# The last stage of a DeltaNet and mLSTM layer takes the mLSTM's product first

## The chip, the cores and the metric

One core of a Trainium2 chip runs the whole program once. The metric is the device time of that execution in microseconds; smaller is better. Three runs of the kernel before gave 989.99, 992.57 and 992.75 us, with a median of 992.57 us. One further execution was taken with the hardware profiler; its time and its trace are used below.

## What is computed

One layer of a backbone over 512 latent tokens (in a row behind 256 context tokens), with 1024 channels. Two mixers read one input projection: a bidirectional gated DeltaNet of 8 heads, whose gated output is `ya`, and a bidirectional mLSTM of 4 heads, whose gated output is `yb`. The part that matters here is the end of the layer:

```
ya = rmsnorm(oa) * silu(z_a)
yb = rmsnorm(hb) * sigmoid(o_b) * silu(z_b)
y  = sigmoid(g_a) * (ya @ w_pa) + sigmoid(g_b) * (yb @ w_pb)
x  = x + gate * (y @ w_out)
out = rmsnorm(x, final_g)
```

`ya` and `yb` are 512 x 1024, and the three weights are 1024 x 1024. The gates `g_a` and `g_b` come from the input projection too, 1024 columns each: 16 dense products of 128 columns, numbered 0 to 15, of which 0 to 7 gate the `ya` product and 8 to 15 the `yb` product.

## The kernel before

Every dense product is done in split precision. A weight chunk of 1024 x 128 is loaded into one of two `raw` buffers (512 KB, queue of SP), ACT casts it into one of three slots of `whs` (line 753, the high part), and DVE subtracts to get `wls` (line 754, the low part). Data has a high and a low part in the same way. One product of 128 columns for 512 tokens is then 24 matmuls of 128x512: for each of 8 blocks of the inner dimension `kt` high by high (line 768), low by high (769) and high by low (770), all into one of two PSUM banks `psd`. A bank is free for the product after next once ACT or DVE has read it.

The mixers come first. Their instructions are not issued as written: a recorder collects them (in the trace they all have line 460), and a list scheduler with a table of costs of its own orders them for each engine. Fillers such as the gate products are handed to it by stretches of a head; the list `G` (line 1529) says how many gate products each of the eight stretches gets. `g_dense` makes one: weights, 24 matmuls, a tanh on ACT into the tile `sg`, and a store of 256 KB to the scratch tensor `sg_d` in DRAM. One gate product is made before the heads and one after the last head, so 14 of the 16 are made there. The last head writes its part of `ya` to `ya_d` and the last mLSTM head its two blocks of `yb` to `yb_d` (scratch in DRAM too).

The last stage (from line 1572 on) is issued as written, though the framework interleaves the engines and gives each engine a fixed order. It has four pieces:

- It loads the 8 blocks of `yb`, then the 8 blocks of `ya`, 256 KB each, into tiles `yld` of which there are three (lines 1585 and 1586), casts each on ACT (line 1587, `ybh` or `yah`) and subtracts on DVE (line 1588, `ybl` or `yal`). A load into a `yld` tile waits until DVE has subtracted from its former tenant.
- `g_last` makes the gate products that are left (14 and 15) with the tanh on ACT into tiles `sgl` (line 1595) that stay on the chip.
- For each of 8 column chunks `n` it takes the `ya` product with `w_pa` and then the `yb` product with `w_pb`. A gate that is not in `sgl` is loaded from `sg_d` (line 1610, two buffers). DVE multiplies the product by the gate (line 1613, tile `yt`), GpSimd adds the two terms (line 1615), ACT and DVE split the sum into `yh` and `yl`.
- Then comes the product with `w_out` (line 1654) and the final norm.

What decides the order around the change is the queue of SP, which issues all loads and stores one after the other and stops at each that has to wait, and the order of ACT and DVE, which stop at each instruction that has to wait.

Of the kernel before, what the change touches and what calls it, by code (L numbers as in the profile page):

```python
# [10 lines left out]
F32 = mybir.dt.float32  # L11
F32R = mybir.dt.float32r
AF = mybir.ActivationFunctionType
ALU = mybir.AluOpType

P = 128
D = 1024
KT = D // P
T = 512
# [473 lines left out]
def hybrid(tc, x, c, ctx_in, c_ctx, ada_w, ada_b, norm_g, w_in, conv_w, a_log, dt_bias,  # L493
           norm_a_g, i_bias, f_bias, norm_b_g, w_pa, w_pb, w_out, final_g, out):
    nc = tc.nc
# [78 lines left out]
    sg_d = dram.tile([2 * KT, P, T], F32, name="sg_d")  # L574
# [29 lines left out]
    nc = rec  # L604
# [9 lines left out]
    ya_d, yb_d, sg_d, gate_d, rows_d = [rec.wrap(t, "DRAM") for t in (ya_d, yb_d, sg_d, gate_d, rows_d)]  # L614
# [127 lines left out]
    def next_slot(n=1):  # L742
        i = slot[0] % NW
        if i + n > NW:
            i = 0
        slot[0] = i + n
        return i

    def split_w(src, c0, wh, wl):

        raw = wpool.tile([P, KT, P], F32, tag="raw", name="raw", bufs=2)
        nc.sync.dma_start(raw, src[:, c0:c0 + P].rearrange("(kt p) n -> p kt n", p=P))
        nc.scalar.copy(wh, raw)  # L753
        nc.vector.tensor_tensor(wl, raw, wh.bitcast(F32), op=ALU.subtract)  # L754

    def load_w(src, c0, at=None):
        i = next_slot() if at is None else at
        split_w(src, c0, whs[:, i], wls[:, i])
        return whs[:, i], wls[:, i]

    def dense_g(w, rh, rl, t0, t1):

        wh, wl = w
        next(between, None)
        ps = psd()
        o = ps[:, 0:t1 - t0]
        for kt in range(KT):
            nc.tensor.matmul(o, wh[:, kt, :], rh[:, kt, t0:t1], start=kt == 0, stop=False)  # L768
            nc.tensor.matmul(o, wh[:, kt, :], rl[:, kt, t0:t1], start=False, stop=False)  # L769
            nc.tensor.matmul(o, wl[:, kt, :], rh[:, kt, t0:t1], start=False, stop=kt == KT - 1)  # L770
            if kt % 2 and kt < KT - 1:
                yield 6 * (t1 - t0) / 2400
        next(between, None)
        return o

    def dense_ch(*args):
        g = dense_g(*args)
        while True:
            try:
                next(g)  # L780
            except StopIteration as e:
                return e.value
# [3 lines left out]
    def seq(*gens):  # L786
        for g in gens:
            yield from g
# [13 lines left out]
    def weave(*streams):  # L802

        live = [[0.0, cost, g] for cost, g in streams]
        while live:
            st = min(live, key=lambda x: x[0] / x[1])
            try:
                st[0] += next(st[2])
            except StopIteration:
                live.remove(st)  # L810
# [527 lines left out]
    def z_dense(h):  # L1338
        w = load_w(win, O_AZ + P * h)
        pz = yield from dense_g(w, hh, hl, TC, TT)  # L1340
        sz = mx.tile([P, T], F32, tag="sz", name="sz", bufs=2)
        nc.scalar.activation(sz, pz, AF.Silu)
        heads[h]["sz"] = sz
        yield 1.28
# [28 lines left out]
    def ml_dense(j):  # L1373
        w = load_w(win, O_BK + P * j)
        k = mx.tile([P, NLC * DVB], F32, tag="mkH", name="mk")[:, 0:TT]
        sck = float(P) ** -0.5
        o = yield from dense_g(w, hh, hl, TC, TT)
        nc.scalar.activation(k[:, TC:TT], o, AF.Copy, scale=sck)
        yield 1.28
        o = yield from dense_g(w, hh, hl, 0, TC)  # L1380
        nc.scalar.activation(k[:, 0:TC], o, AF.Copy, scale=sck)
        yield 0.64
        w = load_w(win, O_BQ + P * j)
        q = mx.tile([P, T], F32, tag="mq", name="mq")
        o = yield from dense_g(w, hh, hl, TC, TT)
        nc.scalar.copy(q, o)
        yield 1.28
        V = mx.tile([P, NCH, DVB + 4], F32, tag="mV", name="mV")
        nc.gpsimd.memset(V[:, :, DVB:DVB + 1], 1.0)
        i = next_slot(2)  # L1390
        for half in range(2):
            load_w(win, O_BV + DVB * j + P * half, at=i + half)
        for ch0 in range(0, NCH, 2):
            ps = psd()
            n = 0
            for ch in range(ch0, ch0 + 2):
                o = ps[:, DVB * (ch - ch0):DVB * (ch - ch0) + DVB]
                tk = slice(P * ch, P * ch + P)
                for kt in range(KT):
                    for a, b in ((hh, whs), (hh, wls), (hl, whs)):  # L1400
                        nc.tensor.matmul(o, a[:, kt, tk], b[:, i:i + 2, kt, :], start=n == 0, stop=n == 2 * 3 * KT - 1)
                        n += 1
                    if kt % 4 == 3:
                        yield 1.28
            nc.scalar.copy(V[:, ch0:ch0 + 2, 0:DVB], ps.rearrange("p (c i) -> p c i", i=DVB))
        ml[j] = (q, k, V)
# [113 lines left out]
    def g_some(n):  # L1520
        for _ in range(n):
            if gn[0] < 2 * KT:
                gn[0] += 1
                yield from g_dense(gn[0] - 1)
# [1 line left out]
    weave((18, gates_g()), (46, seq(qkv(0), g_some(1), qkv(1))))  # L1526
    weave((W_E + W_KV, seq(dn_kv(0), dn_scores(0))), (20.5, qkv(2)))
    weave((W_A2 + W_E, seq(dn_prepa2(0), dn_scores(1))), (33, seq(z_dense(0), ml_dense(0))))
    G = [0, 4, 0, 4, 0, 4, 0, 0]
    for h in range(HA):  # L1530
        j = h // 2
        last = h + 1 == HA
# [21 lines left out]
        if h + 3 < HA:  # L1554
            de.append(qkv(h + 3))
            cost += 20.5
        if G[h]:
            de.append(g_some(G[h]))
            cost += 5.1 * G[h]
        streams = [(wd, seq(*dn)), (cost, seq(*de))]  # L1560
# [7 lines left out]
    nc, ps_d, ps_l, ps_s, ps_o, wpool, cvp, hh, hl, whs, wls, ya_d, yb_d, sg_d, gate_d, cpow = plain  # L1568
# [10 lines left out]
    mg = mgs.enter_context(tc.tile_pool(name="mg", bufs=1, reuse_waits="tile"))  # L1579
    parts = []  # L1580
    for name, src in (("b", yb_d), ("a", ya_d)):
        ph = mg.tile([P, KT, T], F32R, name=f"y{name}h")
        pl = mg.tile([P, KT, T], F32R, name=f"y{name}l")
        for kt in range(KT):
            t = mg.tile([P, T], F32, tag="yld", name="yld", bufs=3)
            nc.sync.dma_start(t, src[P * kt:P * kt + P, :])
            nc.scalar.copy(ph[:, kt, :], t)  # L1587
            nc.vector.tensor_tensor(pl[:, kt, :], t, ph[:, kt, :].bitcast(F32), op=ALU.subtract)
        parts.append((ph, pl))
    sgl = {}  # L1590
# [10 lines left out]
    wo = [(mr.tile([P, KT, HD], F32R, name="woh"), mr.tile([P, KT, HD], F32R, name="wol"))]  # L1601
    wol1 = mr.tile([P, KT, HD], F32R, name="wol1")
    rf = mr.tile([P, 104], F32, name="rf")[:, 0:NLC]
    for n in range(KT):
        terms = []
        for i, ((ph, pl), wsrc) in enumerate(((parts[1], w_pa[0]), (parts[0], w_pb[0]))):
            g = sgl.get(KT * i + n)
            if g is None:
                g = mg.tile([P, T], F32, tag="sg", name="sg", bufs=2)
                nc.sync.dma_start(g, sg_d[KT * i + n])  # L1610
            w = load_w(wsrc, P * n)
            t = mg.tile([P, T], F32, tag="yt", name="yt", bufs=2)
            nc.vector.scalar_tensor_tensor(t, g, 1.0, dense_ch(w, ph, pl, 0, T), op0=ALU.add, op1=ALU.mult)
            terms.append(t)
        nc.gpsimd.tensor_tensor(terms[0], terms[0], terms[1], op=ALU.add)
        nc.scalar.activation(yh[:, n, :], terms[0], AF.Copy, scale=0.5)
        nc.vector.scalar_tensor_tensor(yl[:, n, :], terms[0], 0.5, yh[:, n, :].bitcast(F32), op0=ALU.mult, op1=ALU.subtract)
# [10 lines left out]
    mg = es.enter_context(tc.tile_pool(name="mo", bufs=1, reuse_waits="tile"))  # L1628
# [17 lines left out]
    n = [0] * NLC  # L1646
    for i, c0, c1 in pieces:
        wh, wl = wo[c0 // HD]
        cs, w0, w = slice(c0, c1), c0 % HD, c1 - c0
# [6 lines left out]
        t = mg.tile([P, HD], F32, tag="ot", name="ot", bufs=2)[:, 0:w]  # L1656
# [42 lines left out]
```

## Time and profile before

| | |
|---|---|
| three runs, us | 989.99, 992.57, 992.75 |
| profiled execution, us | 991.41 |
| its span in the trace, us | 989.7 |
| PE busy | 950.6 us, 96% of the span |
| DVE, ACT, POOL busy | 73%, 55%, 22% |
| mean granted clock of PE | 0.989 |

The profile is that of one execution. Its time (991.41) is 1.7 us more than its span, which is what lies around the program. A busy share is of the whole span; PE is the engine that is nearly always busy, so that a change is looked for in the places where PE is idle, or runs below its full clock. Times in the rows are counted from the start of the span.

### The profile page before, as it was taken

Reading aid. Unit: us, or ns where it says so; the run is one execution under the profiler, and the core shown is the slowest. Engines: PE = TensorE matmul, PEld = TensorE weight load, DVE = VectorE, ACT = ScalarE, POOL = GpSimd, SP = SyncE. Lnnn points to the kernel's source line nnn. Section 1 sums busy time; section 2 is a strip of 40 time slices with the busy share of each in tenths; the row PEclk is TensorE's granted clock in tenths of the full one; section 3 lists DMA queues with packets and bytes.
Section 4 is the critical chain, followed back from the end, with each engine's and each line's share of the span. In section 5 each row is a group of like instructions: output and inputs, shape, how many; then the busy total and the mean of one; then the engine's idle time right before and its main releaser. Section 6 shows DMA issues by size and latency. Waiting matters only on the chain.

```text
span 989.7 us, 15262 instructions
## 1 busy us (share of the span) xinstructions
PE 950.6 (96%) x5504; PEld 814.6 (82%) x5504; DVE 722.8 (73%) x1646; ACT 545.4 (55%) x1226; POOL 215.0 (22%) x292
## 2 busy tenths in 40 slices
PE   4999999999989999999999999999999997799996
PEld 2288889887888889988888899888899886688876
DVE  5699688778887877888886777878687655543544
ACT  6566644874675485497356637774655644322322
POOL 2110240320341042134103213220311400011231
PEclk9999999999999999999999999999999999799999
DMA  9822231353412233133122413332223326555562
GB/s 278 266 64 75 67 86 44 86 148 107 114 26 65 75 111 82 44 107 96 43 75 68 124 44 85 84 80 67 91 78 94 75 64 203 169 149 149 149 181 85
DMA packets 133967, 101.49 MB, mean 103 GB/s; under 512 B 6584, under 2 KB 113251, under 8 KB 133893
## 3 DMA queue, kind: packets, MB, share of 16 engines
q1 hardware_dynamic: 133893, 100.53, 36.6%
q8 instruction: 43, 0.70, 0.3%
q14 instruction: 31, 0.25, 0.1%
HBM read 90.49 MB, written 10.03 MB: 102 GB/s over the span
## 4 chain that ended last, share of the span: by engine, by line
PE 90%; DMA 4%; DVE 2%; ACT 2%; issue 1%; POOL 0%; POOLq 0%; SPq 0%; DVEq 0%; ACTq 0%
PE psd L460 51%; PE psl L460 19%; PE pts L460 6%; PE psd L768 3%; PE psd L769 3%; PE psd L770 3%; PE ops L460 3%; PE psd L1654 2%; DMA raw<-in_w_out 1%; DMA yld<-yb_d 1%; DMA prow<-in_norm_a_g 1%; DMA xt<-in_x 1%; DMA yld<-ya_d 0%; DVE wol L754 0%; ACT junk L460 0%
## 5 line engine op out<-in xcount | busy, mean ns | idle before, releaser
L460 PE MATMUL psd<-hh,whs 128*128 128x512 f32 (+1 forms) x720 | 282.7, 393 | 0.0
L460 PE MATMUL psd<-hh,wls 128*128 128x512 f32 (+1 forms) x720 | 268.6, 373 | 0.0
L460 PE MATMUL psd<-hl,whs 128*128 128x512 f32 (+1 forms) x720 | 267.1, 371 | 0.0
L460 PEld LDWEIGHTS psd<-hh,wls 128*128 128x128 f32 x720 | 135.8, 189 | 21.6 <-DVE wls L460 0.3
L460 PEld LDWEIGHTS psd<-hl,whs 128*128 128x128 f32 x720 | 136.3, 189 | 17.4 <-issue 0.9
L460 PEld LDWEIGHTS psd<-hh,whs 128*128 128x128 f32 x720 | 136.3, 189 | 16.5
L460 DVE TENSOR_TENSOR wls<-raw,whs 128x1024 fp32r<-128x1024 f32 x86 | 107.6, 1254 | 15.6 <-ACT whs L460 15.1
L460 ACT CAST whs<-raw 128x1024 fp32r<-128x1024 f32 x86 | 89.9, 1049 | 34.1 <-PE psd L460 25.3
L460 DVE STREAM_TRANSPOSE TL<-TC 32x1024 f32<-32x1024 f32 (+1 forms) x32 | 67.4, 2105 | 6.4 <-POOL TC L460 5.7
L460 DVE TENSOR_TENSOR Z<-Z,tmp 128x30 f32<-128x30 f32 (+7 forms) x240 | 62.4, 260 | 6.0
L460 DVE TENSOR_TENSOR tmp<-TL,Z 128x30 f32<-128x30 f32 (+7 forms) x240 | 61.7, 257 | 6.2
L460 POOL TENSOR_SCALAR_AFFINE_SELECT Mm<-gch 128x384 fp32r<-128x384 f32 x32 | 23.5, 734 | 164.8 <-PE psl L460 117.5
L460 ACT ACTIVATE ud<-pts,C1E 128x128 f32<-128x128 f32 x80 | 28.2, 367 | 54.5 <-PE pts L460 54.2
L460 PE MATMUL psd<-whs,hh 128*128 128x256 f32 x192 | 55.4, 290 | 0.0
L460 PE MATMUL psd<-wls,hh 128*128 128x256 f32 x192 | 54.8, 285 | 0.0
L460 PE MATMUL psd<-whs,hl 128*128 128x256 f32 x192 | 54.4, 284 | 0.0
L460 ACT ACT_TABLE_LOAD x37 | 47.5, 1283 | 1.4 <-PEq L1687 0.8
L460 ACT COPY pad<-psd 128x512 f32<-128x512 f32 (+1 forms) x40 | 20.1, 502 | 48.3 <-PE psd L460 39.1
L753 ACT CAST whs<-raw 128x1024 fp32r<-128x1024 f32 x18 | 19.0, 1053 | 48.9 <-PE psd L769 42.5
L768 PE MATMUL psd<-yah,whs 128*128 128x512 f32 x64 | 26.0, 407 | 11.6 <-ACT yah L1587 11.6
L460 PEld LDWEIGHTS psd<-wls,hh 128*128 128x128 f32 x192 | 36.7, 191 | 0.0
L460 PEld LDWEIGHTS psd<-whs,hl 128*128 128x128 f32 x192 | 36.7, 191 | 0.0
(298 smaller groups left out, 2139.0 us busy)
## 6 DMA issues: line engine op xcount, KB each, us to landing
raw<-in_w_in SPq DMA_DIRECT2D x80, 512.0 KB, 3.9
ada_t<-in_ada_w SPq DMA_DIRECT2D x16, 512.0 KB, 10.1
raw<-in_ada_w SPq DMA_DIRECT2D x8, 512.0 KB, 4.7
Qd<-rows_d SPq DMA_DIRECT2D x16, 256.0 KB, 6.7
raw<-in_w_pa SPq DMA_DIRECT2D x8, 512.0 KB, 4.5
raw<-in_w_pb SPq DMA_DIRECT2D x8, 512.0 KB
raw<-in_w_out SPq DMA_DIRECT2D x8, 512.0 KB, 4.1
sg_d<-sg SPq DMA_DIRECT2D x14, 256.0 KB, 2.4
```

The lines of the kernel that those rows point to most:

```text
L460: getattr(getattr(self.nc, s.eng), s.name)(*a, **k)
L753: nc.scalar.copy(wh, raw)
L768: nc.tensor.matmul(o, wh[:, kt, :], rh[:, kt, t0:t1], start=kt == 0, stop=False)
L769: nc.tensor.matmul(o, wh[:, kt, :], rl[:, kt, t0:t1], start=False, stop=False)
L770: nc.tensor.matmul(o, wl[:, kt, :], rh[:, kt, t0:t1], start=False, stop=kt == KT - 1)
L1654: nc.tensor.matmul(ps, a[:, kt, P * i:P * i + P], b[:, kt, w0:w0 + w], start=m == 0, stop=m == KT * 3 - 1)
```

## The change

There are three edits. In the stretch of the fourth head `G` is 3 where it was 4, so `g_last` makes three gate products (13, 14 and 15) and 13 gates pass through `sg_d`. The tiles `yld` are eight. And the last stage takes the `yb` product ahead of the `ya` product in each chunk, with the `yb` products of chunks 0 and 1 both ahead of the first `ya` product, and with three `yt` tiles.

```diff
-    G = [0, 4, 0, 4, 0, 4, 0, 0]
+    G = [0, 4, 0, 3, 0, 4, 0, 0]
...
-            t = mg.tile([P, T], F32, tag="yld", name="yld", bufs=3)
+            t = mg.tile([P, T], F32, tag="yld", name="yld", bufs=8)
...
+    def term(i, n):
+        (ph, pl), wsrc = ((parts[1], w_pa[0]), (parts[0], w_pb[0]))[i]
+        g = sgl.get(KT * i + n)
+        if g is None:
+            g = mg.tile([P, T], F32, tag="sg", name="sg", bufs=2)
+            nc.sync.dma_start(g, sg_d[KT * i + n])
+        w = load_w(wsrc, P * n)
+        t = mg.tile([P, T], F32, tag="yt", name="yt", bufs=3)
+        nc.vector.scalar_tensor_tensor(t, g, 1.0, dense_ch(w, ph, pl, 0, T), op0=ALU.add, op1=ALU.mult)
+        return t
+
+
+    early = [term(1, n) for n in range(2)]
     for n in range(KT):
-        terms = []
-        for i, ((ph, pl), wsrc) in enumerate(((parts[1], w_pa[0]), (parts[0], w_pb[0]))):
...
-            t = mg.tile([P, T], F32, tag="yt", name="yt", bufs=2)
...
-            terms.append(t)
+        terms = [early[n], term(0, n)] if n < 2 else [term(1, n), term(0, n)]
```

What this does to the order of instructions is shown at three places. The first is the queue of SP where the mixers end and the last stage begins, in the kernel before (`raw` are weight chunks, `yld<-yb_d` and `yld<-ya_d` the loads of the two mixers' outputs):

```order
L752 DMA raw<-in_w_pa 128x8x128
L460 DMA yb_d<-og 128x512 x2
L1586 DMA yld<-yb_d 128x512 x3
L1610 DMA sg<-sg_d 128x512 x2
L1586 DMA yld<-yb_d 128x512 x2
L752 DMA raw<-in_w_pb 128x8x128
L1586 DMA yld<-yb_d 128x512 x3
L752 DMA raw<-in_w_pa 128x8x128
L1586 DMA yld<-ya_d 128x512 x8
```

The same place with the change:

```order
L752 DMA raw<-in_w_pb 128x8x128
L460 DMA yb_d<-og 128x512 x2
L1586 DMA yld<-yb_d 128x512 x8
L1586 DMA yld<-ya_d 128x512 x8
L1609 DMA sg<-sg_d 128x512 x2
L752 DMA raw<-in_w_pa 128x8x128 x2
```

All sixteen loads now stand in one row, and the first two gates and the first two chunks of `w_pa` have moved behind them, while both chunks of `w_pb` that come first are loaded ahead of them.

The second is ACT at the same place, before (`whs<-raw` is the cast of a weight chunk, `sgl<-psd` frees the PSUM bank of a gate product):

```order
L753 CAST whs<-raw 128x1024
L1595 ACTIVATE sgl<-psd 128x512
L1587 CAST ybh<-yld 128x512 x2
L753 CAST whs<-raw 128x1024
L1587 CAST ybh<-yld 128x512
L1595 ACTIVATE sgl<-psd 128x512
L1587 CAST ybh<-yld 128x512 x5
L1587 CAST yah<-yld 128x512 x8
```

And with the change:

```order
L753 CAST whs<-raw 128x1024
L1595 ACTIVATE sgl<-psd 128x512
L1587 CAST ybh<-yld 128x512 x2
L753 CAST whs<-raw 128x1024
L1587 CAST ybh<-yld 128x512 x4
L1595 ACTIVATE sgl<-psd 128x512
L1587 CAST ybh<-yld 128x512 x2
L1587 CAST yah<-yld 128x512 x2
L1595 ACTIVATE sgl<-psd 128x512
L1587 CAST yah<-yld 128x512 x6
L753 CAST whs<-raw 128x1024 x4
```

The second `sgl` stands behind six casts of `yb`, the third behind two of `ya`, and the casts of `w_pa` behind all sixteen.

The third is PE at the seam of the gate products and the merge, before:

```order
L769 MATMUL psd<-hl,whs 128x512
L770 MATMUL psd<-hh,wls 128x512
L768 MATMUL psd<-yah,whs 128x512
L769 MATMUL psd<-yal,whs 128x512
L770 MATMUL psd<-yah,wls 128x512
```

And with the change:

```order
L769 MATMUL psd<-hl,whs 128x512
L770 MATMUL psd<-hh,wls 128x512
L768 MATMUL psd<-ybh,whs 128x512
L769 MATMUL psd<-ybl,whs 128x512
L770 MATMUL psd<-ybh,wls 128x512
```

The first product behind the gates reads `yb` in place of `ya`; 48 such matmuls now run before the first that reads `ya`.

## Rows read from the trace of the kernel before

**Rows 1.** Page, part 1: busy time, share of the span, instructions.
```profile
PE 950.6 (96%) x5504; PEld 814.6 (82%) x5504; DVE 722.8 (73%) x1646; ACT 545.4 (55%) x1226; POOL 215.0 (22%) x292
```

**Rows 2.** Waits of PE, whole span: us in total, times, longest.
```profile
PE psd L768 <- ACT yah L1587: 11.6, 1, 11.6
...
PE psd L1654 <- DVE wol L754: 0.8, 1, 0.8
```

**Rows 3.** Windows: length, busy (instructions) by engine, granted clock, DMA share, GB/s.
```profile
517.00:545.00 28.00, 28.00 (x145) 23.74 (x144) 19.64 (x36) 16.64 (x45) 7.74 (x9) 1.00 0.28 79
545.00:822.90 277.90, 276.69 (x1773) 249.87 (x1772) 209.75 (x541) 164.38 (x430) 61.41 (x92) 1.00 0.30 80
...
835.01:846.66 11.65, 0.00 (x2) 0.00 (x1) 5.08 (x8) 5.56 (x10) 0.00 (x0) 0.65 0.85 253
846.66:852.20 5.54, 5.54 (x13) 4.02 (x13) 3.29 (x5) 2.41 (x5) 0.00 (x0) 0.51 0.58 166
```

**Rows 4.** Chain that ended last, 827 to 846 us: start, us, what.
```profile
827.61 4.32 DMA yld<-yb_d
...
833.40 3.39 DMA yld<-yb_d
...
837.75 3.82 DMA yld<-yb_d
...
842.97 2.85 DMA yld<-ya_d
```

**Rows 5.** Timeline of PE: start, us, engine, line, operation.
```profile
823.00 0.40 PE L768 MATMUL psd<-hh,whs 128*128 128x512 f32 x1
...
846.66 0.79 PE L768 MATMUL psd<-yah,whs 128*128 128x512 f32 x1 [11.65 <-ACT yah L1587]
...
852.20 0.40 PE L769 MATMUL psd<-yal,whs 128*128 128x512 f32 x1
...
860.38 0.39 PE L768 MATMUL psd<-yah,whs 128*128 128x512 f32 x1
...
865.82 0.39 PE L768 MATMUL psd<-ybh,whs 128*128 128x512 f32 x1
```

**Rows 6.** Timeline of SP's queue: start, us of issuing, what.
```profile
825.87 0.38 SPq L752 DMA_DIRECT2D raw<-in_w_pa  x1
826.53 0.98 SPq L460 DMA_DIRECT2D yb_d<-og  x2
827.61 1.68 SPq L1586 DMA_DIRECT2D yld<-yb_d  x3
```

**Rows 7.** Tile yld: durations in ns, min/median/max, first and last start.
```profile
L1587 ACT CAST ybh<-yld x8: 613/618/625, 832.0 to 843.5; 128x512 fp32r<-128x512 f32 x8
L1588 DVE TENSOR_TENSOR ybl<-yld,ybh x8: 683/688/693, 832.7 to 844.2; 128x512 fp32r<-128x512 f32 x8
```

**Rows 8.** Groups by line, 846.6 to 936.8 us: count, busy us, mean ns, idle before.
```profile
L754 DVE TENSOR_TENSOR wls<-raw,whs 128x1024 fp32r<-128x1024 f32 x13 | 18.1, 1392 | 2.2 <-ACT whs L753 2.2
L753 ACT CAST whs<-raw 128x1024 fp32r<-128x1024 f32 x13 | 13.7, 1054 | 36.0 <-PE psd L769 36.0
```

**Rows 9.** Tile sgl: durations in ns.
```profile
L1595 ACT ACTIVATE sgl<-psd x2: 590/590/590, 830.3 to 836.3; 128x512 f32<-128x512 f32 x2
```

**Rows 10.** Windows of the loads, columns as in rows 3.
```profile
828.00:834.00 6.00, 6.00 (x28) 4.95 (x28) 2.52 (x3) 2.76 (x4) 0.00 (x0) 1.00 1.01 362
834.00:838.00 4.00, 1.01 (x5) 0.51 (x3) 2.10 (x3) 3.05 (x5) 0.00 (x0) 1.00 0.71 210
838.00:846.00 8.00, 0.00 (x0) 0.00 (x0) 2.96 (x5) 2.04 (x5) 0.00 (x0) 0.53 0.86 261
```

**Rows 11.** Page, part 6: DMA issues, count, KB each, median us to landing.
```profile
ada_t<-in_ada_w SPq DMA_DIRECT2D x16, 512.0 KB, 10.1
...
raw<-in_w_pa SPq DMA_DIRECT2D x8, 512.0 KB, 4.5
...
yb_d<-og SPq DMA_DIRECT2D x8, 256.0 KB, 2.0
yld<-ya_d SPq DMA_DIRECT2D x8, 256.0 KB, 2.7
```

More of the change, by code (lines that the diff above doesn't have):

```diff
@@ L1603, in hybrid @@
     rf = mr.tile([P, 104], F32, name="rf")[:, 0:NLC]
-    for n in range(KT):
-        terms = []
-        for i, ((ph, pl), wsrc) in enumerate(((parts[1], w_pa[0]), (parts[0], w_pb[0]))):
[L1607 to L1611, printed above, removed]
-            t = mg.tile([P, T], F32, tag="yt", name="yt", bufs=2)
-            nc.vector.scalar_tensor_tensor(t, g, 1.0, dense_ch(w, ph, pl, 0, T), op0=ALU.add, op1=ALU.mult)
-            terms.append(t)
+    def term(i, n):
[9 more added lines that the diff above has]
+    early = [term(1, n) for n in range(2)]
+    for n in range(KT):
+        terms = [early[n], term(0, n)] if n < 2 else [term(1, n), term(0, n)]
         nc.gpsimd.tensor_tensor(terms[0], terms[0], terms[1], op=ALU.add)
```

## The prediction

> **What bounds the kernel now.** I read the busy shares first. PE works 96% of the span [rows 1], so the time is PE's work plus the places where PE stands still or runs at the lower clock. The list of PE's waits then shows one long stop after the start of the program: 11.6 us before the first matmul that reads `yah` [rows 2]. The windows round it show that the mixers ahead leave PE hardly an idle moment (28.00 of 28.00 us busy where head 4's gate products lie, 276.69 of 277.90 from there to the mixers' end), that the stop is 11.65 us long, and that the 5.54 us behind it run at a granted clock of 0.51 [rows 3], which is the lower of its two levels (1.2 in place of 2.4 GHz). The reader should see in the chain of waits what the stop is made of: four loads one behind the other, three of `yb` and one of `ya` (4.32, 3.39, 3.82 and 2.85 us), each started by the subtraction that frees one of three `yld` tiles [rows 4]. PE stands still for `ya`, while `yb`, which is loaded first, lies ready for the product that comes second.
>
> **The change part by part.** One product is the distance between two products' first matmuls at full clock, 865.82 - 860.38 = 5.44 us for 24 matmuls, or 0.227 us each [rows 5].
>
> *The gate product.* Head 4's stretch loses 24 matmuls, 5.44 us of PE, a weight load, a tanh and a 256 KB store; `g_last` gains the same work without the store, and one reload falls away in the merge. Since PE is busy all through that stretch [rows 3], I count the mixers 5.44 us shorter. In the trace the two gate products and eight small transposes take PE from 823.00 to 835.01 [rows 3, 5]; with the change three start at 817.56, take 12.01 + 5.44 = 17.45 us, and end at 835.01 again. By itself this fills the stop only if the mixers do shrink. The saved store and reload hide beside PE and count nothing.
>
> *The order of the products and the eight tiles.* What PE needs at 835.01 is now `yb` block by block, at 840.45 the second `w_pb` product, and at 835.01 + 10.88 = 845.89 the first chunk of `w_pa` and `ya`. All that ends the mixers moves 5.44 us earlier with them, so SP issues the last weight chunk ahead of the `yb` stores at 825.87 - 5.44 = 820.43 and the first `yb` load at 822.17 [rows 6]. The second and third load wait for those stores to land (2.0 us [rows 11]), because their tiles lie where the stored tiles lay; the others follow at 0.56 us each.
>
> ACT comes next, for it takes things in order. Its second weight cast needs the slot of the second gate product, which ends at 835.01 - 5.44 = 829.57. Behind it stand four casts of `yb` and then the `sgl` that frees the bank for the first `yb` product: 829.57 + 1.05 + 4 x 0.62 + 0.59 = 833.7 [rows 7 to 9], 1.3 us before PE wants it. Two more casts of `yb`, two of `ya`, the third `sgl` (after 835.01) and six of `ya` end at about 840.5, and DVE's last subtraction 0.69 us later. Each `ya` load waits for the subtraction of the `yb` block in its tile; the eighth of those ends near 836.1, so the last `ya` load lands near 836.2 + 2.7 = 838.9 [rows 11], before its cast.
>
> Queued behind these sixteen loads on SP are two gates and the first `w_pa` chunk. Three issues of 0.56 us later it is out, near 837.8, and lands 4.5 us later [rows 11], at 842.3; cast and subtraction take 1.05 and 1.39 us [rows 8]: 843.4 and 844.7, against 845.89 for the first matmul and 846.34 for the third, which needs the low part. By bytes: that chunk is the last of 6.29 MB issued since 820.43. At the 362 GB/s that the queue moved when several loads stood in it this takes 17.4 us, at the 261 GB/s of the three-tile rotation 24.1 us [rows 10], landing 844.5 and the low part 0.6 us late. I take no wait, since the new queue is the full kind; both ends stay for the range.
>
> So the stop goes: -11.65 us. With it goes the slow stretch: 12 matmuls start from 846.66 up to 852.20, 5.54 us for what takes 12 x 0.227 = 2.72 at full clock [rows 5], so -2.82 us. Moved instructions on GpSimd and the third `yt` tile cost nothing: the addition of a chunk now follows the `ya` product, the steady part of the merge has PE busy throughout, and each tile is asked for again two products after its last use.
>
> *What may come instead.* The scheduler orders the mixers anew from head 4 on. The trace of before cannot show that order. Its bounds are a gain of the 1.21 us that PE idles there now, and a loss of the whole 5.44 us, if other engines' chains hold head 4's length; I take +0.5, near the present idle share. The wait in the `w_out` stage, 0.8 us [rows 2], may go or double: its loads follow the end of the merge, which moves as a whole. I count it 0.
>
> A rule of the Trainium skill speaks against packing loads. The trace first: the first `yb` load, issued behind a weight chunk and two stores, took 4.32 us, and the first `ya` load 2.85 [rows 4]. "DMA: Bandwidth & Descriptors", section "Latency and other measured facts", gives the access to HBM 0.2 us on average and 2 us at high load. By it the `w_pa` chunk would land up to 1.8 us later, and the sum would be about 0.2 us higher (an estimate); the trace agrees in direction, with 1.5 us between those two loads.
>
> **The sum.** 991.41 - 11.65 - 2.82 + 0.5 = 977.4 us. It is made against the profiled execution, which is 1.2 us below the median of the runs and 1.4 above the lowest of them.
>
> **The rivals.**
> *A: the mixers do not get shorter.* Their chains, DeltaNet scan and mLSTM, would keep head 4's length, and the gate product would be extra work in the last stage. For it: the scans wait on DVE and ACT at every step, and the two fillers per step get thinner. Against it: PE is 28.00 of 28.00 us busy there. Price up to 5.44: 982.3 us.
> *B: the transfers bind.* The first `w_pa` chunk lands as late as the most crowded chunk of this kernel, 10.1 us after its issue [rows 11], at 847.9. The first `ya` product then waits some 3 us; if the clock falls too, another 2.82: 980.4 to 983.3 us. For it: DMA engines are 0.85 busy in the stop [rows 3]. Against it: that crowded chunk is one of sixteen of 512 KB, 8.4 MB, while the burst here has 6.29 MB spread over some 17 us, and 1.6 us of slack lie ahead. In the trace the clock was still 1.00 up to 838, 3 us into the stop [rows 10], so a short wait need not cost the clock.
> *C: the change does not do what it says.* If the tiles of the first loads lie in memory that is freed late, the burst starts late, and the stop stays as long, at best less the product that now fills it: 986 to 991 us.
> *D, slower than before.* The scheduler's costs are its own, and one misjudged step of the scan repeats: heads 4 to 8 have five scans of six chunks, 30 rounds. From 14.0 us of new stops on, 0.47 us in each round, the change loses. For it: ACT and DVE work in order, so one early filler delays a scan step. Against it: an order from the same scheduler left 1.21 us in 277.90 [rows 3]. At 0.6 us a round: 30 x 0.6 = 18 us, 995 us.
>
> **How the numbers follow.** A measurement of this kernel tells 0.3%, about 3 us, from no change. I give the forecast 0.64, A 0.18, B 0.10, C 0.04, D 0.04. The forecast's own spread is 974.5 (no new idle, no wait for `w_out`, a run as low as the lowest) to 980. A, with the late chunk and a run above the profiled one, reaches 984; most of B lies below it too. So 974.5 to 984 leaves out C, D and some of B. Faster by over 0.3%: the forecast, A, B and most of C, 0.94; the same 0.02; slower 0.04.
>
> **What would show it.** Right: no wait of PE for `yah` or `ybh` above 1 us; the clock at 1.00 through the seam; eight `yb` loads issued in about 5 us; the third gate product's end still near 835 us; the merge's 384 matmuls in 87.1 us without a slow start. Wrong: PE waiting for `whs` of the first `w_pa` chunk (B), new waits under the scan's tiles between 500 and 820 us (A, D), or a first `yb` load well after 823 (C). An end of the gate products past 838 would make A true.

## The result and the profile after

| | before | with the change |
|---|---|---|
| median of four runs, us | 991.56 | 974.91 |
| lowest and highest, us | 989.99, 992.75 | 973.84, 975.91 |
| profiled execution, us | 991.41 | 974.75 |
| its span, us | 989.7 | 973.0 |

The ratio is 0.9833, with a 95% interval of 0.9813 to 0.9853. The forecast was 977.4 us, in a range of 974.5 to 984: the kernel came out 2.5 us below the forecast and 0.4 us above the lower end of the range.

The busy shares of the changed kernel, as in [rows 1] (busy time, share of the span, instructions):

```profile
PE 947.0 (97%) x5504; PEld 812.5 (84%) x5504; DVE 728.6 (75%) x1646; ACT 547.0 (56%) x1228; POOL 207.0 (21%) x292
```

PE has the same 5504 matmuls and is busy 3.6 us less, above all because none of them runs at the lower clock in the seam now; the rest of the gain is idle time. PE's waits from 400 us to the end of the span (us in total, times, longest) are a single line. In the same stretch the kernel before has the two of [rows 2] and two in the mixers, 0.9 us for `Vt` and 0.2 us for `R`:

```profile
PE psl L460 <- DVE A L460: 0.4, 1, 0.4
```

There is no wait for `yah` or `ybh` any more, and none in the `w_out` stage. The windows by stage (columns as in [rows 3]) cut the span where PE passes from one stage to the next: the mixers up to 816.58, the three gate products up to 833.82, the two `yb` products up to 844.70, the first `ya` product's start, the rest of the merge up to 921.26, and `w_out`:

```profile
517.00:545.00 28.00, 28.00 (x151) 23.85 (x150) 20.29 (x38) 16.77 (x51) 5.93 (x10) 1.00 0.34 97
545.00:816.58 271.58, 271.11 (x1739) 244.79 (x1737) 209.93 (x536) 161.93 (x421) 59.68 (x90) 1.00 0.30 79
816.58:833.82 17.24, 17.24 (x82) 14.27 (x81) 10.97 (x14) 9.21 (x14) 0.41 (x1) 1.00 0.74 257
833.82:844.70 10.88, 10.88 (x50) 9.01 (x49) 7.18 (x11) 6.25 (x11) 0.00 (x0) 1.00 0.96 294
844.70:847.20 2.50, 2.41 (x11) 1.68 (x10) 1.88 (x3) 1.05 (x1) 0.00 (x0) 1.00 0.21 62
847.20:921.26 74.06, 74.06 (x328) 61.30 (x327) 39.35 (x37) 21.28 (x23) 9.03 (x7) 1.00 0.54 155
921.26:973.00 51.74, 44.05 (x217) 37.24 (x215) 22.40 (x38) 13.50 (x27) 11.91 (x11) 0.95 0.51 142
```

PE goes from the gate products into the merge without a gap, and the clock stays at 1.00 where it was 0.51 to 0.65. For the last two stages of the kernel before the same view gives:

```profile
846.66:936.54 89.88, 89.88 (x385) 73.86 (x385) 43.48 (x47) 26.40 (x31) 13.37 (x7) 0.97 0.51 145
936.54:989.70 53.16, 44.56 (x217) 37.17 (x215) 21.82 (x38) 13.49 (x27) 11.82 (x11) 0.96 0.52 138
```

From these rows the 16.70 us of span are accounted for: mixers 823.00 to 816.58, -6.42; gate products 12.01 to 17.24, +5.23; the stop, -11.65; the merge 89.88 to 87.44, -2.44; the last stage 53.16 to 51.74, -1.42.

How near the transfers came to binding shows in the chain of waits of the changed kernel (start, us, what), between 820 and 846 us:

```profile
820.73 4.24 DMA yb_d<-og
...
827.24 6.01 DMA yld<-yb_d
833.28 0.63 ACT ybh L1587
833.93 0.70 DVE ybl L1588
...
836.12 6.84 DMA raw<-in_w_pa
843.04 1.06 ACT whs L753
844.12 1.24 DVE wls L754
```

The chain runs over the store of `yb`, the last of the eight loads, SP's queue, the first `w_pa` chunk and its low part, which is done at 845.36. In PE's timeline the first `ya` product had already begun by then, and its third matmul, the one that reads `wls`, is some 0.25 us late (0.227 us behind the second would be 845.15):

```profile
833.82 0.39 PE L768 MATMUL psd<-ybh,whs 128*128 128x512 f32 x1
...
844.70 0.39 PE L768 MATMUL psd<-yah,whs 128*128 128x512 f32 x1
844.92 0.39 PE L769 MATMUL psd<-yal,whs 128*128 128x512 f32 x1
845.40 0.50 PE L770 MATMUL psd<-yah,wls 128*128 128x512 f32 x1
```

And SP's queue (start, us of issuing, what), to compare with [rows 6]: the eight `yb` loads follow one another, then the eight `ya` loads, two gates and the `w_pa` chunks:

```profile
820.07 0.98 SPq L460 DMA_DIRECT2D yb_d<-og  x2
821.14 6.53 SPq L1586 DMA_DIRECT2D yld<-yb_d  x8
827.79 7.33 SPq L1586 DMA_DIRECT2D yld<-ya_d  x8
835.18 0.90 SPq L1609 DMA_DIRECT2D sg<-sg_d  x2
836.12 1.37 SPq L752 DMA_DIRECT2D raw<-in_w_pa  x2
...
920.46 0.57 SPq L1636 DMA_DIRECT2D gbc<-gate_d  x1
```

The last line is the first load of the `w_out` stage's own data. It goes out 0.80 us before that stage's first matmul at 921.26. In the kernel before it went out 0.19 us after it (936.54):

```profile
936.73 0.34 SPq L1632 DMA_DIRECT2D gbc<-gate_d  x1
```

### The profile page after: what moved, and what is told of

Same layout as the page of the kernel before. It is cut to its first block, busy times and chain, and to the rows that moved or that the text cites. A ratio compares the mean times of both kernels' runs of the same rounds, so it can differ in the third digit from the quotient of the medians.

```text
span 973.0 us, 15262 instructions
## 1 busy us (share of the span) xinstructions
PE 947.0 (97%) x5504; PEld 812.5 (84%) x5504; DVE 728.6 (75%) x1646; ACT 547.0 (56%) x1228; POOL 207.0 (21%) x292
## 4 chain that ended last, share of the span: by engine, by line
PE 92%; DMA 3%; DVE 2%; issue 1%; ACT 1%; POOL 1%; SPq 0%; POOLq 0%; DVEq 0%; ACTq 0%
PE psd L460 51%; PE psl L460 20%; PE pts L460 6%; PE psd L1658 4%; PE ops L460 3%; PE psd L770 3%; PE psd L768 3%; PE psd L769 3%; DMA raw<-in_w_pa 1%; DMA yld<-yb_d 1%; DMA prow<-in_norm_a_g 1%; DMA xt<-in_x 1%; DMA yb_d<-og 0%; DVE A L460 0%; DVE wts L460 0%
## 5 line engine op out<-in xcount | busy, mean ns | idle before, releaser
L460 PE MATMUL psd<-hh,wls 128*128 128x512 f32 (+1 forms) x712 | 265.1, 373 | 0.0
L460 PE MATMUL psd<-hl,whs 128*128 128x512 f32 (+1 forms) x712 | 264.4, 371 | 0.0
L460 PEld LDWEIGHTS psd<-hh,wls 128*128 128x128 f32 x712 | 134.3, 189 | 21.3 <-DVE wls L460 0.2
L460 PEld LDWEIGHTS psd<-hh,whs 128*128 128x128 f32 x712 | 134.8, 189 | 16.6 <-ACT sz L460 0.5
L460 DVE TENSOR_TENSOR wls<-raw,whs 128x1024 fp32r<-128x1024 f32 x85 | 106.6, 1258 | 14.9 <-ACT whs L460 14.7
L754 DVE TENSOR_TENSOR wls<-raw,whs 128x1024 fp32r<-128x1024 f32 x19 | 28.9, 1521 | 14.7 <-ACT whs L753 14.7
L460 PEld LDWEIGHTS psd<-whs,hh 128*128 128x128 f32 x192 | 36.5, 191 | 0.1
```

Source lines behind the costliest of these rows:

```text
L460: getattr(getattr(self.nc, s.eng), s.name)(*a, **k)
```

## The experiments

Three theories stood at the start. **Theory 1**, the prediction's: PE waits for whatever input stands next in its order, and each of the three edits takes away a part of that wait. **Theory 2**: the eight tiles did it. **Theory 3**: the order of the products did it. The change's three edits give eight combinations; beside the two known kernels all six others ran, and three runs on other questions. The third `yt` tile goes with the new order in every run and was not tried by itself. All are compared with the kernel before, run beside them (medians 991.89, 992.05 and 991.88 us in the three series).

The stages of every profiled execution, as the distance between PE's first matmuls in them, in us (the stop is PE's idle time ahead of the merge; the `w_out` load is `gbc`, against the stage's first matmul):

| | mixers end | gate products and stop | merge | last stage | `gbc` issued | span |
|---|---|---|---|---|---|---|
| before | 823.00 | 12.01 + 11.65 | 89.88 | 53.16 | 0.19 after | 989.7 |
| the change | 816.58 | 17.24 | 87.44 | 51.74 | 0.80 before | 973.0 |
| `order_and_gate` | 816.12 | 17.28 | 88.90 | 52.00 | 0.93 before | 974.3 |
| `tiles_and_gate` | 816.92 | 17.44 + 1.38 | 87.74 | 54.12 | 0.20 after | 977.6 |
| `order_and_tiles` | 822.99 | 11.85 | 89.58 | 52.18 | 0.76 before | 976.6 |
| `order_alone` | 822.92 | 11.85 | 91.46 | 52.17 | 0.81 before | 978.4 |
| `tiles_alone` | 822.72 | 12.03 + 5.50 | 89.08 | 54.17 | 0.19 after | 983.5 |
| `gate_alone` | 816.50 | 17.39 + 8.25 | 89.75 | 53.91 | 0.19 after | 985.8 |
| `two_gates_moved` | 816.08 | 22.74 | 87.50 | 51.88 | 0.96 before | 978.2 |
| `last_chunk_reversed` | 816.67 | 17.27 | 87.63 | 55.13 | 0.19 after | 976.7 |
| `change_again` | 815.36 | 17.25 | 87.92 | 52.87 | 0.80 before | 973.4 |

### One edit undone

**Three tiles in place of eight** (`order_and_gate`), from the changed kernel:

```diff
-            t = mg.tile([P, T], F32, tag="yld", name="yld", bufs=8)
+            t = mg.tile([P, T], F32, tag="yld", name="yld", bufs=3)
```

> The change with three yld tiles in place of eight, everything else of it kept. Theory 1 (PE waits for whatever input stands next, and the order puts 48 matmuls, 10.9 us, ahead of ya): the three-tile chain took 17.3 us from the first yb load to the eighth block of yb (827.6 to 844.9); started at 821.1 it ends near 838.4, and PE needs that block at 833.8 + 4.8 = 838.6, so yb causes at most a wait of 1 us; ya's last block comes 11.2 us later, near 849.6, where PE wants it at 849.5. Time 975 to 979 us. Theory 2 (the eight tiles are what removes the stop): the rotation is back, a stop of 4 to 6 us and a slow stretch stay, 981 to 986 us.

Measured: 976.86 us, ratio 0.9849 [0.9827, 0.9872]. PE starts the merge on time and stops once, inside the first `ya` product:

```profile
PE psd L768 <- ACT yah L1587: 1.6, 1, 1.6
```

Theory 1's time is met, though the wait came for `ya` and not, as it had it, for `yb`; theory 2 falls, for without the eight tiles 15.0 of the 16.6 us remain.

**The old order** (`tiles_and_gate`), the kernel before with `G` 3 in the fourth head and eight tiles:

```diff
-    G = [0, 4, 0, 4, 0, 4, 0, 0]
+    G = [0, 4, 0, 3, 0, 4, 0, 0]
...
-            t = mg.tile([P, T], F32, tag="yld", name="yld", bufs=3)
+            t = mg.tile([P, T], F32, tag="yld", name="yld", bufs=8)
```

> The kernel before with eight yld tiles and the gate product moved, the merge still in the old order (ya first). Theory 1: the gates end near 833.8; the first block of ya is cast and subtracted near 835.2 and the others follow at 0.69 us, about as fast as PE takes them (0.68), so the stop is 1.5 to 3 us and the clock stays up: 976 to 979 us. Theory 3 (the order of the products is what removes the stop): PE still stands for ya behind all of yb, stop over 5 us, 981 to 986 us.

Measured: 978.78 us, ratio 0.9861 [0.9839, 0.9883].

```profile
PE psd L768 <- ACT yah L1587: 1.4, 1, 1.4
...
PE psd L1654 <- DVE wol L754: 0.8, 1, 0.8
...
PE psd L1654 <- DVE ot L1657: 0.7, 1, 0.7
```

The stop is nearly gone although `ya` is still wanted first, so theory 3 falls too. What this kernel lacks beside the change is 1.4 us of stop, and 2.4 us in the last stage (54.12 against 51.74), where nothing was edited: the first sign of a term that the prediction did not have.

**The gate product back in head 4** (`order_and_tiles`), from the changed kernel:

```diff
-    G = [0, 4, 0, 3, 0, 4, 0, 0]
+    G = [0, 4, 0, 4, 0, 4, 0, 0]
```

> The change with the gate product put back into the fourth head's stretch (G has 4 there), so two gate products are left at the end. Theory 1: PE reaches the merge 5.4 us earlier after the last mixer's outputs are written. yb's eighth block comes 1 to 2 us late, and the first w_pa chunk, which lands some 22 us after the yb stores, comes 4 to 6 us late: 979 to 982 us, with a wait of PE on the w_pa cast. Theory 2 or 3 (the tiles, or the order, are enough, and the moved gate product is worth nothing because it is only moved): 974 to 976 us.

Measured: 978.21 us, ratio 0.9865 [0.9845, 0.9885]. The time came out just under theory 1's range and above that of theories 2 and 3, and the wait is not where it was expected: PE did not stop for `w_pa`, but took 13.33 us for the two `yb` products (834.84 to 848.17) where the change took 10.88, as the blocks of `yb` came in late. PE's list shows it in part:

```profile
PE psd L769 <- DVE ybl L1588: 0.8, 1, 0.8
```

With only two gate products to cover them, the `yb` loads themselves are late, and the wait they cause leaves time for the chunk behind them. The product moved to the last stage therefore works as cover for the first loads. That PE waits for what stands next in its order holds; which input that would be was expected wrongly.

### One edit alone

**The gate product alone** (`gate_alone`), the kernel before with the `G` line of the change.

> The kernel before with only the gate product moved. Theory 1: the mixers end some 6.4 us earlier, the three gate products fill up to about 834 us, and the three-tile chain, which starts 6.4 us earlier too, lets the first ya block come at 840: a stop of about 6 us, 984 to 986 us. Rival (moved work is only moved): 990 us or more.

Measured: 988.53 us, ratio 0.9971 [0.9958, 0.9983], a gain of 3.4 us, a few us less than theory 1 wanted and more than its rival. The stop fell from 11.65 to 8.25, and ACT's timeline shows the likely reason that it fell no further:

```profile
834.49 1.04 ACT L753 CAST whs<-raw 128x1024 fp32r<-128x1024 f32 x1 [3.13 <-DMA raw<-in_w_pa]
835.44 1.65 ACT L1587 CAST ybh<-yld 128x512 fp32r<-128x512 f32 x3
...
841.48 1.86 ACT L1587 CAST yah<-yld 128x512 fp32r<-128x512 f32 x3 [3.88 <-DMA yld<-ya_d]
```

ACT waits 3.13 us for a weight chunk with three casts of `yb` behind it, and these casts free the three tiles into which `ya` is loaded. Longer cover is worth little while the loads wait for the tiles: with eight tiles in both kernels the same edit gains 6.8 us by the medians (13.1 against 6.3).

**The eight tiles alone** (`tiles_alone`), the kernel before with the `bufs` line of the change.

> The kernel before with only eight yld tiles. Theory 1: the first block of ya is there some 6 us after PE has ended the two gate products (841 to 842 us in place of 846.7) and the others follow at 0.7 us: stop of 6 to 7 us, 983 to 987 us. Theory 2 (the tiles remove the stop): stop under 3 us, 977 to 981 us. Theory 3 (the order does): 990 us or more.

Measured: 985.74 us, ratio 0.9942 [0.9924, 0.9961]. The stop and the stretch behind it, in the windows (columns as before):

```profile
834.70:840.25 5.55, 0.05 (x2) 0.00 (x1) 5.11 (x8) 5.28 (x10) 0.00 (x0) 0.76 1.00 354
840.25:845.00 4.75, 4.75 (x12) 3.58 (x13) 4.01 (x8) 3.68 (x7) 0.00 (x0) 0.57 0.90 319
```

The DMA engines are fully busy in the stop (1.00, 354 GB/s): the stop is now spent at the full rate of the transfers, where the rotation through three tiles had them at 0.85 and 253 GB/s [rows 3]. Theory 1's time is met, with a stop of 5.5 us where it had 6 to 7; theories 2 and 3 fall.

**The order alone** (`order_alone`), the changed kernel with four gate products in head 4 and three tiles.

> The kernel before with only the new order of the products (and the third yt tile). Theory 1: PE reaches the merge at 835 us; yb's eighth block comes at 844 to 845 us by the three-tile chain, so the first product is spread to about 845, and ya's blocks follow until 859 to 860; the w_out products start some 6 us later than with the moved gate product (922.3 us there): 981 to 985 us. Theory 3 (the order alone removes the stop): 975 to 979 us. Theory 2 (the tiles do): 988 us or more.

Measured: 980.10 us, ratio 0.9881 [0.9866, 0.9896], a gain of 12.0 us, the largest of the single edits, 1 us beyond theory 1's range and short of theory 3's, so that neither time is met. PE's waits from 820 to 930 us:

```profile
PE psd L768 <- ACT yah L1587: 1.0, 2, 0.5
PE psd L769 <- DVE yal L1588: 0.3, 1, 0.3
PE psd L769 <- DVE ybl L1588: 0.2, 1, 0.2
```

One long stop has become many short ones: the merge takes 91.46 us where 384 matmuls at 0.227 us would take 87.1. The listed waits are 1.5 us of these 4.4; the rest lies in gaps too short for the list, for PE starts only 94 matmuls (21.3 us of work) in the 25.23 us from 834.77 to 860. The clock stayed at 1.00 from 823 to 926 us, so the slow stretch is saved in full.

In gain over the kernel before the single edits give 12.0 (order), 6.3 (tiles) and 3.4 us (gate), 21.6 in sum; the pairs 15.0 (order and gate), 13.7 (order and tiles) and 13.1 (tiles and gate); all three 16.4 to 16.6. All shorten the same stop, but they replace one another only in part. The order and the tiles do: 18.3 us added up, 13.7 together. The order and the gate product simply add (15.4 and 15.0). The tiles and the gate product give at least their sum (9.7 and 13.1), for together they make the stop so short (1.38 us) that the merge has no slow start: 87.74 us, against 89.08 and 89.75 with one of them. The third edit adds some 1.5 to 3.5 us to a pair.

### Where the unforeseen part came from

**The last chunk in the old order** (`last_chunk_reversed`), from the changed kernel. By now a theory for the last stage stood: its tiles lie in memory of the `yb` blocks, and since `ya` is now taken last, that memory is free one product before the merge ends, so that its loads start earlier. Reversing the eighth chunk alone takes that away:

```diff
-        terms = [early[n], term(0, n)] if n < 2 else [term(1, n), term(0, n)]
+        terms = [early[n], term(0, n)] if n < 2 else [term(1, n), term(0, n)] if n < KT - 1 else [term(0, n), term(1, n)]
```

> The change, but in the last of the eight chunks the ya product comes before the yb product, so that yb's tiles are read to the very end of the merge. Theory (the seven loads of 512 KB for the final stage go into memory that the yb tiles leave; with ya last that memory is free one product early): the loads start again 0.2 us after the w_out products begin, not 0.8 us before, PE waits for the last w_out chunks, and the last stage takes 53 to 54 us in place of 51.7: 1 to 2 us more than the unchanged kernel of the same call. Rival (the tail gained by chance, or by other loads): the last stage stays at 51.7 to 52 us and the time within 0.5 us.

Measured: 977.95 us, ratio 0.9859 [0.9842, 0.9876], 2.3 us more than the unchanged kernel beside it. PE's waits from 915 us on, where the change has none:

```profile
PE psd L1658 <- DVE ot L1661: 1.2, 1, 1.2
PE psd L1658 <- DVE wol L754: 0.8, 1, 0.8
PE psd L1658 <- ACT woh L753: 0.4, 1, 0.4
```

`gbc` goes out 0.19 us after the stage's first matmul again, at 921.76, and the stage takes 55.13 us:

```profile
921.76 0.34 SPq L1636 DMA_DIRECT2D gbc<-gate_d  x1
```

The table bears it out over all executions: where `ya` is last, `gbc` goes out 0.76 to 0.96 us ahead and the last stage takes 51.74 to 52.87 us, 52.1 in the mean (six executions); where `yb` is last, it goes out behind and the stage takes 53.16 to 55.13 us, 54.1 in the mean (five).

The waits of SP's queue show what holds `gbc` back, in the kernel before and with the last chunk reversed:

```profile
SPq L1632 <- PE psd L770: 1.0, 1, 1.0
...
SPq L1636 <- PE psd L770: 1.2, 1, 1.2
```

In all five executions with `yb` last SP waits 1.0 to 1.2 us for the last matmuls of the merge; in none of the six with `ya` last does it. There `gbc` goes out right behind the `w_out` chunks that stand ahead of it on SP (issued up to 920.40 in the change), so that memory which is free a whole product sooner, 5.44 us, lets the loads start only 1 us earlier. How 1 us of earlier loads is worth some 2 us of the stage is not shown; 1.7 of the 2.3 us stand in PE's waits of the stage (2.4 us here, 0.7 in the run below).

**The changed kernel again** (`change_again`), unaltered, as the measure for that run.

> The change as it is, beside the others on the same chip: 974 to 976 us, the last stage at 51.7 us and the mixers' end at 816.6 us again.

Measured: 975.62 us, ratio 0.9839 [0.9823, 0.9855]. The mixers ended at 815.36, 1.2 us earlier than expected, and the last stage took 52.87 with a wait of 0.7 us for `wol` that the first profile did not have. Single stages thus move by about 1 us from one execution to the next; the terms below are to be read with that in mind.

**A second gate product moved** (`two_gates_moved`), from the changed kernel, in search of a faster one: four gate products in the last stage as cover, and 24 matmuls fewer in head 6.

```diff
-    G = [0, 4, 0, 3, 0, 4, 0, 0]
+    G = [0, 4, 0, 3, 0, 3, 0, 0]
```

> The change with a second gate product moved, from the sixth head's stretch to the last stage (four left at the end). Theory 1: there is no stop left to fill, PE's work is the same: within 1.5 us of the change, 973.5 to 976.5 us. Rival (the mixers shrink by more than the product that leaves them, 6.4 us for 5.44 in the change's trace, because the fillers get in the way of the scans): another 1 us or more off, 972 to 973.9 us.

Measured: 982.19 us, ratio 0.9899 [0.9876, 0.9921]: slower than the change by about 7 us, and both expectations missed. The profiled execution, 980.14 us, is the fastest of the four; it is 5.4 us above the change's, and what the others add no trace shows. The mixers end only 0.5 us earlier (816.08). The window from 545 us to there shows the time that was to be saved as idle time of PE:

```profile
545.00:816.08 271.08, 267.15 (x1707) 239.94 (x1706) 207.28 (x533) 159.61 (x415) 61.45 (x89) 1.00 0.29 76
```

PE's waits from 400 to 820 us (the change has only 0.4 us for `A` there):

```profile
PE psl L460 <- DVE A L460: 2.6, 3, 1.2
PE psl L460 <- DVE W L460: 0.6, 1, 0.6
...
```

PE is idle for 3.93 us in that window, against 0.47 with the change, and 3.65 of it lies behind 750 us. Where the time went shows in SP's stores of the heads' outputs, here those of the sixth and seventh head, then the same two with the change:

```profile
695.89 0.34 SPq L460 DMA_DIRECT2D ya_d<-sz  x1
...
747.07 0.32 SPq L460 DMA_DIRECT2D ya_d<-sz  x1
...
704.17 0.32 SPq L460 DMA_DIRECT2D ya_d<-sz  x1
...
759.80 0.32 SPq L460 DMA_DIRECT2D ya_d<-sz  x1
```

The sixth head, in whose stretch the product was left out, is done 8.28 us earlier and the seventh 12.73 us, but the eighth, at 816.60 against 817.09, only 0.49 us. (The fourth head, ahead of the edit, was already 1.00 us earlier in this execution.) The time is lost in the eighth head, where PE waits for the matrices from which that head's scan is prepared:

```profile
761.65 0.91 PE L460 MATMUL psl<-A,Dm 128*128 128x128 f32 x6 [0.83 <-DVE A L460]
...
770.61 0.91 PE L460 MATMUL psl<-A,Dm 128*128 128x128 f32 x6 [1.18 <-DVE A L460]
```

So the sixth head did get done sooner, and the eighth gave the time back. That it had too little other work left to put beside its own chain is the likely reason; no run shows it by itself. No version faster than the change was found.

## Why the prediction was right, and where it was not

**The stop, -11.65: right.** PE takes `yb` when the gate products end, with the `sgl` that frees its bank done 1.5 us ahead (832.28 against 833.82; 1.3 was worked out). The three pairs show that it takes any two of the edits to remove nearly all of it, and no single one did. One reading under it was wrong: when PE stopped at 835.01, `yb` did not lie ready for its product. Its last block was split only at 844.9 us (844.2 + 0.69 [rows 7]), and with the order alone the merge indeed lost 4.4 us to late blocks. Also, only three of the four loads of [rows 4] were started by a subtraction; the first, at 827.61, went out behind the stores of `yb` [rows 6].

**The slow stretch, -2.82: right, less 0.38.** The merge is 2.44 us shorter. Most of the difference is the wait for the low part of the first `w_pa` chunk, counted at none: 0.25 us here, 0.5 in the second profile. The step that failed was the landing, taken as 4.5 us from [rows 11]. The chunk took 6.84 us, behind sixteen loads and at a DMA share of 0.96; it was issued 1.7 us earlier than worked out, but PE came for it 1.2 us earlier too (844.70 against 845.89), so that it was the 1.6 us of slack that took up most of the delay. The other end that the prediction kept, the bytes at the 261 GB/s of [rows 10] with a low part 0.6 us late, was the better guide. The eight `yb` loads took 6.5 us to issue, not 5, since SP waited for the stores of `yb`: 4.24 us in the chain, where the median of [rows 11] gave 2.0.

Here the rule of the Trainium skill that spoke against packing loads ("DMA: Bandwidth & Descriptors", section "Latency and other measured facts": 0.2 us for the access to HBM on average, 2 us at high load) agrees in direction and about in size, with 2.3 us more for that chunk than the median; whether it was that access or the queue no run here tells apart.

**The gate product, -5.44, +0.5 and +5.44: the mis-sized term.** The last stage's part was +5.23. The mixers became 6.42 us shorter where 4.94 was counted: PE has 5.58 us less to do between 545 us and their end, and its idle time there fell from 1.21 to 0.47 us, where I had added 0.5. Over all executions the mean end of the mixers is 816.36 us with three gate products in head 4 (six executions, the one with head 6 altered left out) and 822.91 with four (four of them), 6.5 us apart. The order that the scheduler gives after the change is thus a little tighter: the waits for `Vt` and `R` (0.9 and 0.2 us) stand in all four executions with four products and in none with three, which have 0.3 to 0.4 us for `A`. Why the scheduler's order does so was not tried.

**The last stage, 0: wrong in its reason.** "Its loads follow the end of the merge, which moves as a whole" is the step that failed. The first of the loads waits for the last reader of the memory that it goes to (1.0 us for PE in SP's queue before), and the change altered which product that is. It is worth 1.42 us in the profile, 2.3 us when it was taken away by itself, and 2.0 between the means of the six and the five executions.

**The sum.** -13.97 was forecast and -16.70 measured; the 2.73 between them are the last stage (1.42), the mixers (1.48) and the gate products (0.21), less 0.38 in the merge. The first two were gains, where nothing or a small loss had been counted. The range held by 0.4 us only: its lower end allowed for no new idle time, no wait in `w_out` and a run as low as the lowest, but for no gain beyond that.

**The rivals.** A falls: the mixers got 6.42 us shorter. With a second product moved they got only 0.5 us shorter still, and not because the head that lost it kept its length: the eighth head held the end. The argument against A, that PE is busy all through the stretch, would have spoken for that move as well, for before the change PE is as busy in what follows (109.01 of 110.00 us from 640 to 750 and 72.68 of 72.90 from there to the mixers' end): a full busy share does not tell whether the end will follow when work is taken out. B came near: the chain that ended last runs over the transfers, but at 0.25 to 0.5 us, and the clock did not fall. C falls with the first `yb` load at 821.14, D with no new wait above 0.4 us in the scans.

## What to carry to other kernels

When an engine stops for an input at a seam, three things shorten the stop: to take the input that comes first, to give the loads more tiles, and to put work that needs none of it ahead. Their gains must not be added unseen: here two of them replaced each other in part (18.3 us added up, 13.7 together), while the cover gained 6.8 us where the loads had tiles enough and 3.4 where they waited for them. Work moved out of a stretch pays only if what comes behind it can move up too, and a busy share near 100% does not tell: the chain of a later stretch can hold the end. And whoever reorders the last products of a stage changes which memory is free first, and with it when the next stage's loads can start.

## What the runs showed of the hardware

PE's granted clock bore short waits: with the order alone, four waits of 0.2 to 0.5 us in the 25 us behind 835, and a stop of 1.55 us in `order_and_gate`, left it at 1.00. A stop of 5.5 us (`tiles_alone`) brought it to 0.57 in the 4.75 us behind it, one of 11.65 us to 0.51.

In a burst of loads a single transfer took much longer than its median in the kernel before [rows 11]: the 256 KB store of `yb` 4.24 us against 2.0, the 512 KB chunk of `w_pa` 6.84 against 4.5. Whether the place in the burst or the load on the memory made them late no run tells apart.
